# Column strips of the modulation products, chained into whole groups on TensorE

## Chip, core and metric

The kernel runs on one core of a Trainium2 chip. The metric is the device time of one execution in microseconds. Three timed runs of the kernel before gave 1551.01, 1553.77 and 1553.95 us; their median, 1553.77 us, is the time that the change is held against.

## What is computed

Two models run one after the other on the same 256 tokens of width 1024. The first block has two layers of four parallel mixers (latent attention, differential attention, a top-k attention, a short convolution), each between a normalisation, an input projection and an output projection. The second block has two layers with a mixer and a mixture of 16 experts; its shifts, scales and gates come from a *modulation* vector, which depends on the inputs `c` and `c_ctx` alone:

```python
def second_block(x, c, ctx, c_ctx, ada_w, ada_b, ...):
    silu_c = jax.nn.silu(c)
    silu_cc = jax.nn.silu(c_ctx)
    x_lat, x_ctx = x, ctx
    for l in range(DEPTH):
        mod_lat = (silu_c @ ada_w[l] + ada_b[l])[:, None, :]
        mod_ctx = (silu_cc @ ada_w[l] + ada_b[l])[None, None, :]
        sh1, sc1, g1, sh2, sc2, g2 = jnp.split(mod_lat, 6, axis=-1)
...
def reference(...):
    x = first_block(...)
    return second_block(x, ...)
```

Two rows (`c` and `c_ctx`) go through a 1024 x 6144 matrix in each of two layers: much weight, little arithmetic.

## The kernel before

The program is written with a tile framework whose scheduler simulates the engines and takes, on each engine, the ready instruction that stands first in priority; each engine then runs its instructions strictly in the order in which they were put. An order edge (`issue_after`) says only that one instruction stands behind another on its engine. `high_priority(n)` moves what it encloses n places ahead in priority.

**First block.** Weights come in units of 128 x 2048 float32 (1 MB) into a ring of three buffers called `w` (`stream`, L353). Each unit is split by ScalarE (`wh`, L373) and VectorE (`wl`, L374) into a high and a low part, and TensorE multiplies high by high, high by low and low by high (`mm3`): these are the `pf` and `pt` products of the input and output projections. Between them stand the products of the mixers: `ixp`, `uq`, `ukv`, `lgA`, `lgB`, `poA` and others.

**Modulation.** The weights of the modulation, 48 loads of 1 MB, go through the same ring (`wload`, L347). The generator `ada_chunks` (L941) loads one such buffer for each k and issues four products from it. Each has the 32 columns of `cT` as its stationary operand (two of them in use) and 512 columns of weight moving, and writes another 32 partitions of one PSUM bank: the four products stand in four column strips of TensorE's array. Two k are summed in the bank and then added to `adab` by VectorE (L952). The generator is drawn from by `fill` (L966) at 12 places of each first layer, one step of two k at each, as work for TensorE between the mixers' products. In the kernel before, the four products of a buffer are issued by a plain loop, with no edge between them:

```python
for t in range(4):
    self.mm(ps[32 * t:32 * t + 32], self.cT[:, k], w[:, t], k % ADAK == 0, k % ADAK == ADAK - 1)
```

so the scheduler is free to put another ready product between two strips.

**Groups that were chained already.** `side_by_side` (L274) issues the products of several streams, interleaved, with an order edge from each to the next, for products that stand in different strips of the array or in different rows of it: `cmb`, `lgN`, `poN` and `lgC` in the second block's first mixer (L1210 to L1342), `yc` in the last mixture of experts (L1993). Within each round the streams are issued in falling order (`reversed(group)`). The edges keep the order, not the neighbourhood: other products may stand in between.

After the first block come the second block's first mixer (neighbourhood attention and an mLSTM, some 400 to 760 us), a mixture of experts with gathered rows (to some 1085 us), the second mixer and the last mixture of experts.

Of the kernel before, what the change touches and what calls it, by code (L numbers as in the profile page):

```python
# [31 lines left out]
XBUFS = 3  # L32
ADA = "pj"
FILLP = 1
MIX = (1, 1, 0, 0)
XL = (0, 1)
XN = (lambda nc: nc.gpsimd, lambda nc: nc.gpsimd)
ADAK = 2
# [196 lines left out]
class Emit:  # L235
# [37 lines left out]
    def side_by_side(self, *streams, banks=(), after=None):  # L273

        one = self.cst["ones"][:, :1]
        for m in [(b[:1, :1], one, one, True, True) for b in banks] + [m for group in zip(*streams) for m in reversed(group)]:
            with self.tc.issue_after(after) if after else ExitStack():
                after = self.mm(*m).ins  # L280
        return after

# [652 lines left out]
    def ada_chunks(self, pool):  # L935

        nc, io = self.nc, self.io
        for l in range(2):
            ab = pool.tile([P, 3, 512], F32, tag="adab", name="adab")
            with self.tc.issue_after(self.rooted):  # L940
                nc.gpsimd.memset(ab, 0.0)  # L941
                for w in range(2):
                    nc.gpsimd.dma_start(ab[w:P:32], io["ada_b"][l])
            for m in range(3):
                for k in range(KD):
                    if k % ADAK == 0:
                        ps = self.psum(ADA, name="ada")
                    w = self.wload(io["ada_w"][l, m, :, k], [P, 4, 512])
                    for t in range(4):
                        self.mm(ps[32 * t:32 * t + 32], self.cT[:, k], w[:, t], k % ADAK == 0, k % ADAK == ADAK - 1)  # L950
                    if k % ADAK == ADAK - 1:
                        nc.vector.tensor_add(ab[:, m], ps, ab[:, m])  # L952
                    if k == KD - 1 and m == 2:
                        for w in range(2):
                            v = self.mod[l][w:w + 1].rearrange("o (m t j) -> (o t) m j", m=3, t=4)
                            nc.gpsimd.dma_start(v, ab[w:P:32])
                    if k % 2:
                        yield

    def fill(self, n=1):  # L960
        for _ in range(n):
            with self.tc.high_priority(FILLP):
                next(self.filler, None)
# [923 lines left out]
    def moe_onehot(self, l, NT):  # L1887
# [4 lines left out]
        with ExitStack() as ctx:  # L1892
# [89 lines left out]
            def back(pr, owT, Y, after=None):  # L1982
                for t in range(NT):

                    pos = [self.psum(POT[j], name="yc") for j in range(2)]
                    r = [slice(64 * j, 64 * j + 64) for j in range(2)]
                    after = self.side_by_side(*([(pos[j], owT[r[j], t, i], Y[i][n][r[j]], i + n == 0, i + n == 2)
                                                 for i in range(2) for n in range(2)] for j in range(2)), after=after)
                    for j in range(2):
                        js = slice(j * 512, (j + 1) * 512)  # L1990
                        o = self.x[:, t, js]
                        nc.vector.tensor_add(o, o, pos[j])  # L1992
                        if pr == NE // 2 - 1:  # L1993
                            (nc.sync, nc.scalar)[j].dma_start(self.out[t * P:(t + 1) * P, js], o)
# [4 lines left out]
            for e, (w13, w2) in enumerate(weights):  # L1999
                pr = e // 2  # L2000
                ph = self.psum("pj", name="ph")
                if e == NE - 1:
                    step = second(e - 1, *todo)
                    for k in range(0, KD, 2):
                        last = hidden(e, tiles[pr][0], w13, k, ph, 2)
                        if k == 0:
                            back(pr - 1, tiles[pr - 1][1], Ys[-2:], last.ins)
                        for _ in range(MIX[k // 2]):
                            with self.tc.issue_after(last.ins):
# [82 lines left out]
```

## Time and profile before

| | before |
|---|---|
| median of three timed runs | 1553.77 us |
| the profiled execution | 1563.38 us, span 1561.6 us |
| TensorE (PE) busy | 1413.6 us, 91% |
| VectorE (DVE) busy | 716.0 us, 46% |
| ScalarE (ACT) busy | 438.9 us, 28% |
| GpSimd (POOL) busy | 158.0 us, 10% |
| modulation products (`ada`), union of their spans | 73.2 us |
| mean granted TensorE clock | 0.945 of full speed |
| weight loads of the modulation | 48 of 1024 KB, 4.9 us to landing |

The profiled execution took 1563.38 us, 0.6% more than the median. The page gives busy time as the union of the spans of an engine's instructions. Matmuls are pipelined and their ends are modelled, so the length of one product says little; what one costs is read from the start of one to the start of the next. A float32 product leaves two records in the trace: 192 `ada` products are 384 records.

### The profile page before, as it was taken

What the parts mean: (1) busy time and instruction counts of PE and PEld (TensorE: products, weight loads), DVE (VectorE), ACT (ScalarE), POOL (GpSimd) and SP (SyncE); (2) the same over time, 40 slices, a digit from 0 to 9 for tenths busy, and PEclk for the clock granted to TensorE, in tenths of its full rate; (3) what the DMA queues carried; (4) which work ended last, traced back from release to release, by engine and by line L of the source; (5) the groups of instructions that cost most, each with busy time, mean ns of one, the idle gap of its engine ahead of it and who ended that gap; (6) DMA issues with size and microseconds to landing.
All of it is one profiled execution on the core that took longest, in us unless ns stands there. A gap on an engine that the chain in (4) does not pass through costs nothing.

```text
span 1561.6 us, 24557 instructions
## 1 busy us (share of the span) xinstructions
PE 1413.6 (91%) x10118; PEld 926.5 (59%) x10118; DVE 716.0 (46%) x1609; ACT 438.9 (28%) x881; POOL 158.0 (10%) x217
## 2 busy tenths in 40 slices
PE   8999999999999998989569999888538998999997
PEld 7576787768888994959523333333138685443442
DVE  4756545856654546365511111111076655333433
ACT  4334332344543324243201111111034442111110
POOL 2100120002100221000110000000143000000000
PEclk9999999999999996999789999999759998999998
DMA  8677675676623111205589888777553517999990
GB/s 295 233 295 285 229 252 174 233 276 237 217 84 96 55 55 39 70 28 216 217 302 330 300 305 338 287 304 300 199 221 109 222 38 284 421 421 422 380 405 31
DMA packets 65703, 359.23 MB, mean 230 GB/s; under 512 B 13027, under 2 KB 16349, under 8 KB 26793
## 3 DMA queue, kind: packets, MB, share of 16 engines
q1 hardware_dynamic: 57680, 335.04, 57.5%
q0 software_dynamic: 5824, 19.68, 3.9%
q10 hardware_dynamic: 2073, 2.79, 0.5%
q8 instruction: 84, 1.38, 0.4%
q14 instruction: 42, 0.34, 0.1%
HBM read 344.77 MB, written 12.71 MB: 229 GB/s over the span
## 4 chain that ended last, share of the span: by engine, by line
PE 35%; DMA 8%; DVE 3%; issue 2%; ACT 1%; POOL 1%; SPq 0%; ACTq 0%; POOLq 0%; DVEq 0%
PE ph L270 13%; PE py L270 6%; DMA w<-in_w_dram 5%; PE pt L270 4%; PE pq L270 3%; DMA ybuf<-ysq 2%; PE gtp L294 1%; PE yc L270 1%; PE px L270 1%; PE pyq L270 1%; PE lgG L270 1%; PE poG L270 1%; PE xtp L294 1%; DMA X<-hbuf,tab 1%; DVE x L1992 1%
## 5 line engine op out<-in xcount | busy, mean ns | idle before, releaser
L270 PE MATMUL ph<-w,XT 128*64 128x512 f32 x1024 | 250.6, 611 | 17.8 <-DMA w<-in_w_dram 14.9
L374 DVE TENSOR_TENSOR wl<-w,wh 128x2048 fp32r<-128x2048 f32 (+2 forms) x74 | 151.8, 2058 | 87.1 <-ACT wh L373 86.8
L270 PE MATMUL pt<-wh,hT 128*128 128x256 f32 x640 | 185.0, 290 | 3.5 <-ACT wh L373 2.0
L270 PE MATMUL pt<-wl,hT 128*128 128x256 f32 x640 | 184.0, 289 | 0.0
L270 PE MATMUL pt<-wh,hTl 128*128 128x256 f32 x640 | 183.2, 290 | 0.6 <-DVE hTl L374 0.2
L373 ACT CAST wh<-w 128x2048 fp32r<-128x2048 f32 (+2 forms) x74 | 126.6, 1719 | 122.9 <-PE pt L270 44.9
L270 PEld LDWEIGHTS ph<-w,XT 128*64 128x64 f32 x1024 | 71.2, 138 | 139.6 <-issue 120.0
L270 PE MATMUL pf<-hTl,wh 128*128 128x256 f32 (+1 forms) x480 | 141.6, 296 | 0.0
L270 PE MATMUL pf<-hT,wh 128*128 128x256 f32 (+1 forms) x480 | 141.3, 298 | 0.3
L270 PE MATMUL pf<-hT,wl 128*128 128x256 f32 (+1 forms) x480 | 140.3, 293 | 0.7 <-DVE wl L374 0.7
L1758 DVE SCALAR_TENSOR_TENSOR ga<-ga,ph 64x512 f32<-64x512 f32 x32 | 21.8, 680 | 258.8 <-ACT ga L1757 258.8
L270 PEld LDWEIGHTS pt<-wh,hT 128*128 128x128 f32 x640 | 123.2, 193 | 9.6 <-ACT wh L373 2.5
L270 PEld LDWEIGHTS pt<-wl,hT 128*128 128x128 f32 x640 | 123.0, 192 | 4.6 <-issue 3.4
L270 PEld LDWEIGHTS pt<-wh,hTl 128*128 128x128 f32 x640 | 121.7, 192 | 5.2 <-issue 3.8
L270 PE MATMUL py<-w,gT 128*64 128x512 f32 x512 | 121.8, 605 | 0.8 <-DVE gT L1831 0.8
L270 PEld LDWEIGHTS pf<-hT,wh 128*128 128x128 f32 x480 | 91.5, 192 | 11.1 <-issue 4.7
L270 PEld LDWEIGHTS pf<-hT,wl 128*128 128x128 f32 x480 | 92.0, 192 | 6.8 <-issue 2.7
L270 PEld LDWEIGHTS pf<-hTl,wh 128*128 128x128 f32 x480 | 92.1, 192 | 5.6 <-issue 4.4
L270 PEld LDWEIGHTS py<-w,gT 128*64 128x64 f32 x512 | 36.1, 138 | 68.5 <-issue 65.2
L270 PE MATMUL ada<-w,cT 128*32 128x512 f32 x384 | 73.2, 612 | 1.3 <-DMA w<-in_ada_w_dram 1.3
L270 PE MATMUL pq<-w,XT 128*32 128x256 f32 x1024 | 72.1, 386 | 0.0
L270 PE MATMUL pt<-wh,yT 128*128 128x256 f32 x256 | 63.7, 293 | 0.0
(527 smaller groups left out, 2139.7 us busy)
## 6 DMA issues: line engine op xcount, KB each, us to landing
w<-in_w_dram SPq DMA_DIRECT2D x192, 1024.0 KB, 15.5
w<-in_ada_w_dram SPq DMA_DIRECT2D x48, 1024.0 KB, 4.9
w<-in_w_in_dram SPq DMA_DIRECT2D x30, 1024.0 KB, 6.9
w<-in_even_w_dram SPq DMA_DIRECT2D x12, 1024.0 KB, 6.2
w<-in_w_out_dram SPq DMA_DIRECT2D x8, 1024.0 KB, 5.0
w<-in_even_out_dram SPq DMA_DIRECT2D x4, 1024.0 KB
ybuf<-ysb SPq DMA_DIRECT2D x16, 256.0 KB
w<-in_odd_w_dram SPq DMA_DIRECT2D x4, 1024.0 KB
```

What stands on the lines that cost most here:

```text
L270: self.last = self.nc.tensor.matmul(out, lhsT, rhs, start=start, stop=stop)
L294: self.nc.tensor.transpose(out, in_, self.cst["ident"][:k, :k])
L373: self.nc.scalar.copy(hi, src)
L374: (self.nc.vector if eng == "v" else self.nc.gpsimd).tensor_tensor(out=lo, in0=src, in1=hi.bitcast(F32), op=ALU.subtract)
L1758: nc.vector.scalar_tensor_tensor(g, g, 1.0, ph[0:n], op0=ALU.add, op1=ALU.mult)
L1992: nc.vector.tensor_add(o, o, pos[j])
```

## The change

The four products of a modulation buffer go through `side_by_side`: an order edge from each to the next, in falling order of the strips. And in `side_by_side`, for all its callers, every product behind the first of a group is lifted by 20000 places in priority, so that a group once begun is taken on as soon as its next product is ready.

```diff
+GROUPP = 20000
...
         one = self.cst["ones"][:, :1]
-        for m in [(b[:1, :1], one, one, True, True) for b in banks] + [m for group in zip(*streams) for m in reversed(group)]:
-            with self.tc.issue_after(after) if after else ExitStack():
+        ms = [(b[:1, :1], one, one, True, True) for b in banks] + [m for group in zip(*streams) for m in reversed(group)]
+        for n, m in enumerate(ms):
+            with ExitStack() as c:
+                if after:
+                    c.enter_context(self.tc.issue_after(after))
+                if n:
+                    c.enter_context(self.tc.high_priority(GROUPP))
                 after = self.mm(*m).ins
         return after
...
                     w = self.wload(io["ada_w"][l, m, :, k], [P, 4, 512])
-                    for t in range(4):
-                        self.mm(ps[32 * t:32 * t + 32], self.cT[:, k], w[:, t], k % ADAK == 0, k % ADAK == ADAK - 1)
+                    self.side_by_side(*([(ps[32 * t:32 * t + 32], self.cT[:, k], w[:, t], k % ADAK == 0, k % ADAK == ADAK - 1)]
+                                        for t in range(4)))
```

No product, load or copy is added or removed. What moves is the order. On TensorE, in the first layer's latent attention (`ixp`, `uq` and `ukv` are its and the top-k attention's products; the number behind `w_` is the buffer's), the kernel before has

```order
L270 MATMUL ada_518<-w_519,cT_116 32x512
L270 MATMUL ixp_532<-s4a_364,s2a_459 128x512
L270 MATMUL ada_518<-w_519,cT_116 32x512 x3
L270 MATMUL ada_518<-w_525,cT_116 32x512
L270 MATMUL ixp_544<-s4a_364,s2a_459 128x512
L270 MATMUL ada_518<-w_525,cT_116 32x512 x3
L270 MATMUL ada_658<-w_659,cT_116 32x512
L270 MATMUL uq_673<-s8a_204,wuq_154 128x256
L270 MATMUL ada_658<-w_659,cT_116 32x512
L270 MATMUL uq_673<-s8a_204,wuq_154 128x256
```

and the changed kernel at the same place

```order
L271 MATMUL ada_518<-w_519,cT_116 32x512 x4
L271 MATMUL ixp_532<-s4a_364,s2a_459 128x512
L271 MATMUL ada_518<-w_525,cT_116 32x512 x4
L271 MATMUL ixp_544<-s4a_364,s2a_459 128x512
L271 MATMUL ada_658<-w_659,cT_116 32x512 x4
L271 MATMUL uq_673<-s8a_204,wuq_154 128x256 x4
```

The strips of one buffer now stand together, and the four `uq` products behind them too. Over the whole program the 192 products stood in 61 uninterrupted runs: 22 of one product, 4 of two, 8 of three, 18 of four, 2 of five and 7 of eight. Now they stand in 37 runs: 26 of four and 11 of eight (two buffers behind each other).

On TensorE at the start of the first output projection (`pf` is a product of the input projection, `pt` of the output projection), the kernel before has, of the eight strips of two buffers, one among `pf` products further ahead and the other seven in five runs:

```order
L270 MATMUL pf<-hT,wl 128x256
L270 MATMUL ada<-w,cT 32x512 x2
L270 MATMUL pt<-wh,yT 128x256
L270 MATMUL ada<-w,cT 32x512 x2
L270 MATMUL pt<-wl,yT 128x256
L270 MATMUL pt<-wh,yTl 128x256
L270 MATMUL ada<-w,cT 32x512
L270 MATMUL pt<-wh,yT 128x256
L270 MATMUL ada<-w,cT 32x512
L270 MATMUL pt<-wl,yT 128x256
L270 MATMUL ada<-w,cT 32x512
L270 MATMUL pt<-wh,yTl 128x256
```

and the changed kernel

```order
L271 MATMUL pf<-hTl,wh 128x256
L271 MATMUL pf<-hT,wl 128x256
L271 MATMUL ada<-w,cT 32x512 x4
L271 MATMUL pt<-wh,yT 128x256
L271 MATMUL pt<-wl,yT 128x256
```

One buffer's four strips stand whole ahead of the projection; the other buffer's four stand where the single strip stood before. The order of the weight loads on SyncE's queue is the same up to the end of the first block. In the second block the `yc` products stand in 25 runs where there were 27, one group of four `lgC` is cut into one and three, and `pt`, `qk` and `pom` products of the first mixer change places.

## Rows read from the trace of the kernel before

**Rows 1.** Page, the span in 40 equal slices, busy tenths of TensorE.

```profile
PE   8999999999999998989569999888538998999997
```

**Rows 2.** Windows by stage: length, busy us of each engine, granted clock, DMA share, GB/s.

```profile
0.00:405.00 405.00, 393.77 (x2667) 292.37 (x2668) 242.57 (x597) 157.28 (x282) 49.05 (x74) 0.99 0.71 250
...
560.00:780.00 220.00, 188.92 (x1360) 153.63 (x1358) 123.46 (x318) 73.32 (x168) 25.21 (x34) 0.89 0.29 106
780.00:1085.00 305.00, 279.65 (x2324) 109.64 (x2324) 45.73 (x86) 35.90 (x84) 15.52 (x16) 0.95 0.84 311
1085.00:1561.00 476.00, 397.88 (x2564) 231.60 (x2562) 217.60 (x436) 114.23 (x240) 43.22 (x48) 0.91 0.66 261
```

**Rows 3.** Waits of TensorE from 20 to 405 us: total, times, longest.

```profile
PE htp L270 <- ACT idx L315: 3.5, 2, 3.3
PE ada L270 <- DMA w<-in_ada_w_dram: 1.3, 1, 1.3
```

**Rows 4.** Timeline of TensorE, first layer: start us, us, instructions, records.

```profile
45.82 1.05 PE L270 MATMUL ada<-w,cT 128*32 128x512 f32 x2
46.79 1.12 PE L270 MATMUL ixp<-s4a,s2a 128*128 128x512 f32 x2
47.85 1.07 PE L270 MATMUL ada<-w,cT 128*32 128x512 f32 x8
48.84 1.12 PE L270 MATMUL ixp<-s4a,s2a 128*128 128x512 f32 x2
...
50.90 0.70 PE L270 MATMUL uq<-s8a,wuq 128*128 128x256 f32 x2
51.52 1.05 PE L270 MATMUL ada<-w,cT 128*32 128x512 f32 x2
52.50 0.70 PE L270 MATMUL uq<-s8a,wuq 128*128 128x256 f32 x2
...
57.96 1.89 PE L270 MATMUL uq<-s8a,wuq 128*128 128x256 f32 x8
59.78 1.06 PE L270 MATMUL ada<-w,cT 128*32 128x512 f32 x8
```

**Rows 5.** The same timeline, two buffers behind each other.

```profile
71.82 1.92 PE L270 MATMUL ada<-w,cT 128*32 128x512 f32 x16
73.68 0.33 PE L294 MATMUL ptp<-cpack,p 128*128 128x128 f32 x1
```

**Rows 6.** The same timeline, three strips and the fourth, among projection products.

```profile
114.44 1.06 PE L270 MATMUL ada<-w,cT 128*32 128x512 f32 x6
115.43 0.38 PE L270 MATMUL pf<-hT,wh 128*128 128x256 f32 x1
115.74 1.05 PE L270 MATMUL ada<-w,cT 128*32 128x512 f32 x2
116.72 0.38 PE L270 MATMUL pf<-hTl,wh 128*128 128x256 f32 x1
116.94 0.28 PE L270 MATMUL pf<-hT,wl 128*128 128x256 f32 x1
117.06 0.28 PE L270 MATMUL pf<-hT,wh 128*128 128x256 f32 x1
```

**Rows 7.** The same timeline, a group behind an idle stretch, and one that waited.

```profile
224.53 1.94 PE L270 MATMUL ada<-w,cT 128*32 128x512 f32 x8
226.39 1.22 PE L270 MATMUL htp<-idx,x 128*128 128x128 f32 x4
...
338.47 1.06 PE L270 MATMUL ada<-w,cT 128*32 128x512 f32 x8 [1.27 <-DMA w<-in_ada_w_dram]
```

**Rows 8.** Windows of 5 us, columns as in rows 2.

```profile
65.00:70.00 5.00, 5.00 (x20) 3.12 (x20) 4.97 (x23) 2.27 (x9) 0.14 (x1) 1.00 0.19 79
...
80.00:85.00 5.00, 5.00 (x44) 5.00 (x44) 5.00 (x7) 1.58 (x1) 0.00 (x0) 1.00 1.02 424
```

**Rows 9.** Waits of all engines from 20 to 405 us.

```profile
ACT wh L373 <- DMA w<-in_w_in_dram: 21.8, 8, 5.6
```

**Rows 10.** Waits of SyncE's queue up to 420 us.

```profile
SPq L362 <- PE ada L270: 87.8, 27, 11.6
```

## Prediction, made before the changed kernel ran

> **What bounds the kernel now.** I read the page's slices first: TensorE is at eight or nine tenths almost everywhere [rows 1]. The windows by stage say where that means something. The first block, up to some 405 us, keeps TensorE busy for 393.8 of 405 us at a granted clock of 0.99 [rows 2], 2.4 GHz nearly throughout, while VectorE works 243 us, ScalarE 157 us and the DMA engines 71% of the time. What TensorE waits for there, by the view of waits, comes to little: 3.5 us on ScalarE at the start of the second layer and a single wait of 1.3 us on a modulation load [rows 3]. So the first block is TensorE's own queue: a microsecond taken out of it ends the block a microsecond earlier, as long as the other engines and the loads keep up. Busy alone would not show that, since ends of matmuls are modelled; the waits do. The stages behind, from 560 us, have idle TensorE time in each, 31, 25 and 78 us by the same windows [rows 2], and follow on the first block's result.
>
> The modulation products are all in the first block. What one costs depends on its neighbours. One strip alone: from 51.52 to the next instruction at 52.50, 0.98 us [rows 4]. Four strips together: from 47.85 to 48.84, 0.99 us [rows 4]. Three: 0.99 us, and the fourth, cut off by one `pf` product, another 0.98 us [rows 6]. Eight, that is two buffers: 71.82 to 73.68, 1.86 us [rows 5]. A run of one to four strips costs the same: strips that stand together run at the same time, and a strip alone takes the time of four.
>
> **The change, term by term.** *Fewer runs.* The order counts 22, 4, 8, 18, 2 and 7 runs of one, two, three, four, five and eight. From these rows I price one and two at 0.98, three and four at 0.99, five and eight at 1.86 us: 26 x 0.98 + 26 x 0.99 + 9 x 1.86 = 68.0 us. Now 26 runs of four and 11 of eight: 25.7 + 20.5 = 46.2 us. The difference is **21.8 us** less. (Two runs were longer than their price, the one at half the clock, 1.86 us for four strips, and the one that waited [rows 7]; I leave both as they are.)
>
> *Fewer switches.* A run also slows what is next to it. From the `pf` at 115.43 to the second `pf` behind the strip, 116.94, it is 1.51 us [rows 6]; take off the run of 0.98 and two ordinary steps of 0.12 (116.94 to 117.06), and 0.29 us are left for going in and out. Among `uq`: from 50.90 to 52.50 it is 1.60 us; the run is 0.98, one `uq` product among its own is a quarter of 57.96 to 59.78, 0.46 [rows 4], which leaves 0.16. There are 24 runs fewer (61 to 37): 3.8 to 7.0 us, of which I take the middle, **5.4 us**, since both neighbourhoods are common.
>
> *The falling order of the strips, and the edges.* No instruction and no semaphore wait that the profile shows. Taken as nothing; the price if the overlap suffers is a rival below. The Trainium skill (TensorE: Matmul & The Clock Gate, Why this matters for your kernels) speaks against a full gain: three column tiles of 512 columns ran 2.38 times as fast as one after the other, not three times. By that figure, an estimate, a group would cost 3 x 0.98 / 2.38 = 1.23 us and not 0.99, and the changed runs some 59 us, so that 9 of the 21.8 us were left. The trace disagrees: three strips took 0.99 us against 0.98 for one [rows 6], 2.97 times; I go by the rows.
>
> *What loses its cover.* 27.2 us go out of a block in which VectorE, ScalarE and the loads do the same work as before. Averages leave room: VectorE would be at 243 of some 378 us, the DMA engines at 0.76. But there are tight places. Around 65 to 85 us VectorE works through the top-k search, 4.97 to 5.00 of each 5 us [rows 8]; TensorE has to come to its results some 5 us earlier there, and most of the chain in front of them also starts earlier, since the `uq` products that it waits for are no longer spread among strips. The DMA engines swing between 79 and 424 GB/s in the same stretch [rows 8]: loads go out when a ring buffer comes free, often by an `ada` product itself (27 waits of the queue for it, 87.8 us in all [rows 10]), and then three go at once. ScalarE's casts waited 21.8 us for projection weights [rows 9], all of it hidden behind queued products. Where two buffers are now used in one run, the second load has to be there 1 us after the first. Bounds: below, the one wait of 1.3 us goes too (a gain); above, each of the other 10 runs of eight waits like the one at 338.47 [rows 7], 10 x 1.27 = 12.7 us of loss. One of seven such runs waited so far, so the nearest row speaks for some 2 us, and I add as much for VectorE: **4 us** of loss.
>
> *The second block.* The groups that were chained before gain no work and lose none; the two runs of `yc` that go are worth at most 2 x 0.29 us in a stage with 78 us of idle TensorE time, taken as nothing. The changed places of `pt`, `qk` and `pom` in the first mixer can cost or give back some of the 31 us that TensorE idles there [rows 2]; a tenth of it, 3 us either way, is my estimate, and zero my value. Everything behind the first block waits for its result, and the weights of the experts for buffers that the first mixer frees, so I expect the stages to move as a whole: the DMA engines run at 0.29 from 560 to 780 us [rows 2], so no stream runs ahead there that would stay where it is.
>
> **Sum:** 21.8 + 5.4 - 4 = 23.2 us less. The profiled execution took 1563.4 us, so it would come to 1540.2; the median of the timed runs lies 0.6% below, which changes 23.2 by 0.1, so the timed kernel should take 1553.8 - 23 = **1531 us**. A difference of 0.2%, 3 us, is about what a measurement of this kernel can tell from none.
>
> **Rivals.**
> *The cover runs out (0.14).* Loads or VectorE's searches end last in more places than I allow and take back about half: 10 runs of eight at 1.27 us each, 1553.8 - 27.2 + 12.7 = 1539 us, up to 1549. For it: the swings of the DMA engines and VectorE's full stretches [rows 8]. Against it: one load wait in 48 groups so far [rows 3], and a gain spread over 380 us.
> *The strips overlap only in part in falling order (0.06).* A group then costs between 0.99 us and the 0.98 us of each strip alone. At a quarter more, 1.23 us, the sum is 1553.8 - 9 - 5.4 + 4 = 1543 us; were the overlap lost altogether, 144 more strips at nearly 1 us each would make it slower by over 100 us, which I give no share. The Trainium skill's 2.38 (the page named above) would be this case. Against it: three strips in 0.99 us [rows 6], if in rising order.
> *The gain is given back later (0.04).* A stage behind ends by something that did not move, and the time stays at 1554 us. For it: the expert stage runs at 311 GB/s with DMA share 0.84 [rows 2]. Against it: its loads start from buffers that the mixer in front frees.
> *Slower: the ring of weight buffers becomes the bound (0.04).* TensorE runs in order, so a group that stands whole before its load has landed holds up everything behind it, where a single strip further back did not yet have to start. It decides if the mean wait of the 48 groups exceeds 27.2 / 48 = 0.57 us; if each of the 37 runs waited 1.27 us as at 338.47 [rows 7], that is 47 us and the kernel takes 1574 us. Against it: the DMA share of 0.71 [rows 2].
>
> **Chances and range.** My forecast, with a gain of 15 to 32 us, has 0.72. Faster by over 0.2% are it and the first two rivals, 0.92; within 0.2% the third, 0.04; slower the last, 0.04. The range runs from 1521 us (no wait added, the upper price of switches, 3 us gained in the mixer: 21.8 + 7.0 + 1.3 + 3 = 33) to 1546 us, which takes in the partial overlap and most of the case where the cover runs out.
>
> **What would show it.** The 384 `ada` records in 37 runs, each run of four at 0.99 us from its start to the next instruction and each of eight at 1.86; their union down from 73.2 to about 50 us; the first block's end near 382 us with TensorE still busy in nearly all of it; the stages behind as long as before. Wrong would be: records of one group that start half a microsecond apart (no overlap); waits of `ada` on its load, or of `pf` and `pt` on `wl`, of more than 10 us in the first block; or a first block shorter by 23 us with an end that is not.

## The result, and the profile after

The changed kernel took 1535.83 us (median of five runs, 1533.85 to 1542.31) against 1553.77 us before: 0.9889 times, 95% interval 0.9858 to 0.9921. The prediction was 1531.0 us, 1521 to 1546. The profiled execution took 1533.85 us, span 1532.1 us.

The slices of the page, as [rows 1], and the windows by stage, as [rows 2] (the first stage now ends at 385, the others are 20 us earlier):

```profile
PE   8999989999899998989399999888358998999997
```

```profile
0.00:385.00 385.00, 370.81 (x2677) 290.81 (x2678) 240.70 (x595) 154.05 (x276) 46.40 (x72) 0.99 0.72 263
540.00:760.00 220.00, 185.20 (x1364) 153.24 (x1362) 124.44 (x321) 73.49 (x168) 25.25 (x35) 0.91 0.29 106
760.00:1065.00 305.00, 283.20 (x2349) 110.97 (x2349) 48.44 (x93) 37.34 (x88) 15.40 (x16) 0.97 0.84 315
1065.00:1532.00 467.00, 389.98 (x2537) 228.74 (x2537) 214.91 (x429) 112.42 (x236) 43.17 (x48) 0.91 0.67 264
```

The same work now fits in a first stage that is 20 us shorter, with TensorE idle for 14 us of it (385 less 370.8) where it was 11. DMA share and GB/s rose little: the loads follow the ring.

The `ada` products come in the 37 runs that the order showed. The timeline of TensorE at the places of [rows 4] and [rows 5], one run that waited, and the half-clock run that answers to [rows 7]:

```profile
47.85 1.07 PE L271 MATMUL ada<-w,cT 128*32 128x512 f32 x8
48.84 1.13 PE L271 MATMUL ixp<-s4a,s2a 128*128 128x512 f32 x2
...
51.06 1.99 PE L271 MATMUL uq<-s8a,wuq 128*128 128x256 f32 x8
...
68.32 1.92 PE L271 MATMUL ada<-w,cT 128*32 128x512 f32 x16
70.18 0.92 PE L271 MATMUL lgA<-ks,qs 128*128 128x128 f32 x4
...
120.49 1.06 PE L271 MATMUL ada<-w,cT 128*32 128x512 f32 x8
122.78 1.06 PE L271 MATMUL ada<-w,cT 128*32 128x512 f32 x8 [1.23 <-DMA w<-in_ada_w_dram]
...
218.95 1.94 PE L271 MATMUL ada<-w,cT 128*32 128x512 f32 x8
220.82 1.22 PE L271 MATMUL htp<-idx,x 128*128 128x128 f32 x4
```

A run of four costs 0.99 us from start to next, one of eight 1.86. At 122.78 the second buffer of a run of eight came late. The four `uq` products stand together at 51.06, as the order said.

What TensorE waits for from 20 to 385 us, the counterpart of [rows 3]:

```profile
PE htp L271 <- ACT idx L321: 3.3, 1, 3.3
PE ada L271 <- DMA w<-in_ada_w_dram: 2.5, 3, 1.2
PE pt L271 <- DVE wl L380: 2.0, 2, 1.2
PE pf L271 <- DVE wl L380: 0.5, 1, 0.5
```

Two things are new: three waits for modulation loads where there was one (two of them inside runs of eight, for the second buffer, as the prediction feared), and waits of the output projection (`pt`) for `wl`, the low parts of its weights, where there was none. (The second layer's projection lies behind 385 us and has two more; the page's costliest groups put 4.0 us of idle time ahead of `pt<-wl,yT` to `wl` over the whole program, 3.2 of it up to 420 us.)

### The profile page after: what moved, and what is told of

The parts are those of the page before. It is cut to its first block, busy times and chain, and to the rows that moved or that the text cites. A ratio compares the mean times of both kernels' runs of the same rounds, so it can differ in the third digit from the quotient of the medians.

```text
span 1532.1 us, 24552 instructions
## 1 busy us (share of the span) xinstructions
PE 1380.1 (90%) x10118; PEld 919.8 (60%) x10118; DVE 714.3 (47%) x1609; ACT 438.1 (29%) x881; POOL 154.2 (10%) x217
## 4 chain that ended last, share of the span: by engine, by line
PE 35%; DMA 8%; DVE 3%; ACT 1%; issue 1%; POOL 1%; SPq 1%; ACTq 0%; POOLq 0%; DVEq 0%
PE ph L271 14%; PE py L271 6%; DMA w<-in_w_dram 5%; PE pt L271 4%; PE pq L271 3%; DMA ybuf<-ysq 3%; PE yc L271 1%; PE gtp L300 1%; PE px L271 1%; PE pyq L271 1%; PE lgG L271 1%; PE poG L271 1%; PE xtp L300 1%; DVE x L1998 1%; ACT wh L379 0%
## 5 line engine op out<-in xcount | busy, mean ns | idle before, releaser
L271 PEld LDWEIGHTS pt<-wh,hT 128*128 128x128 f32 x640 | 123.4, 193 | 10.6 <-issue 4.2
L271 PE MATMUL pt<-wl,yT 128*128 128x256 f32 x192 | 54.6, 286 | 4.0 <-DVE wl L380 4.0
```

The source lines that it names most:

```text
L271: self.last = self.nc.tensor.matmul(out, lhsT, rhs, start=start, stop=stop)
```

## Where the time went: a landmark

The `mg` products stand early in the second block and wait for the first block's result. Their start splits an execution in two. The rows of that tile (minimum, median and maximum length in ns, first and last start in us), for the kernel before in two executions and the changed kernel, one fence each:

```profile
L270 PE MATMUL mg<-hT,wmg x64: 272/273/297, 464.2 to 467.4; 128*32 128x128 f32 x64
```

```profile
L270 PE MATMUL mg<-hT,wmg x64: 272/273/297, 462.4 to 465.6; 128*32 128x128 f32 x64
```

```profile
L271 PE MATMUL mg<-hT,wmg x64: 272/273/297, 444.6 to 447.8; 128*32 128x128 f32 x64
```

All runs with this landmark, but for resident, which stands with its experiment; "behind" is the span of the profiled execution less the start of `mg`. Each ratio is to runs of the kernel before on the same chip.

| kernel | median (range), us | ratio [95%] | `mg` | behind |
|---|---|---|---|---|
| before, first profile | 1553.77 | | 464.2 | 1097.4 |
| before_again | 1555.42 (1549.0 to 1561.2) | 1.0000 [0.9979, 1.0021] | 462.4 | 1088.9 |
| changed | 1535.83 (1533.9 to 1542.3) | 0.9889 [0.9858, 0.9921] | 444.6 | 1087.5 |
| after_again | 1537.49 (1532.2 to 1543.9) | 0.9883 [0.9846, 0.9920] | 446.3 | 1088.4 |
| edges_only | 1558.69 (1553.3 to 1564.4) | 1.0014 [0.9990, 1.0038] | 464.0 | 1095.4 |
| lift_only | 1554.82 (1552.2 to 1562.9) | 1.0000 [0.9978, 1.0021] | 461.5 | 1090.0 |
| cover | 1548.08 (1545.3 to 1553.7) | 0.9965 [0.9946, 0.9984] | 454.0 | 1091.0 |
| no_edges | 1543.01 (1537.1 to 1549.5) | 0.9931 [0.9905, 0.9957] | 444.6 | 1102.0 |
| first_only | 1533.43 (1532.5 to 1534.9) | 0.9872 [0.9856, 0.9887] | 444.0 | 1088.6 |
| rising | 1542.35 (1537.6 to 1544.6) | 0.9922 [0.9905, 0.9938] | 445.0 | 1097.9 |
| cover2 | 1539.12 (1534.3 to 1545.8) | 0.9916 [0.9893, 0.9939] | 444.9 | 1091.8 |
| lift_no_edge | 1537.97 (1537.2 to 1538.9) | 0.9899 [0.9883, 0.9916] | 444.3 | 1091.1 |

The changed kernel reaches `mg` 16.1 to 19.6 us earlier, by either pair of profiles. What lies behind stays at 1087.5 to 1088.9 us in three of these four profiles; the first profile of the kernel before was long there, and the kernel before alone thus shows 1089 and 1097 us. So the gain is the first block's. A single `mg` is good to some 3 us: before, before_again and lift_only have the same order in the first block, and their `mg` runs from 461.5 to 464.2.

## Experiments

**The two kernels again.** No edit.

> The unchanged kernel before. The two profiles compared so far differ by 29.5 us of span while the timed medians differ by 17.9 us, and the profile of before was 9.6 us above its median. Theory: the change is worth 19 to 20 us in the first block (start of the first gate product mg at 464.2 us before, 444.6 after) and nothing behind it, and the profile of before was simply a long execution in its later stages. Then this profile has mg again within 1 us of 464.2 us, 61 ada runs, and a span near 1552 us, the difference of some 9 us to the first profile lying behind 470 us. Rival: the change also shortens the later stages by some 10 us; then this profile's stages behind 470 us are as long as in the first profile of before (1097 us from mg to the end). Ratio of times: 1.00 within 0.003 by either.

> The changed kernel again. Theory: mg within 1 us of 444.6 us, 37 ada runs, time 1533 to 1540 us, ratio 0.987 to 0.991; what varies from run to run lies behind the first block. Rival (the change acts on the later stages too): the stretch from mg to the end stays at 1087 us or below, where before has 1097.

Measured: table. The times and the counts of runs came out as expected; `mg` missed the 1 us that was allowed, 1.8 us early in before_again and 1.7 us late in after_again. The rival, later stages shortened by the change, fell: before_again has 1088.9 us behind `mg`. In before_again the 61 runs took 68.8 us in sum, each counted from its start to the next instruction, with no wait; in the changed kernel the 37 runs took 49.7, of which 2.1 are waits for loads. (The third load wait, 0.3 us, stands ahead of a run and not in it.) Without waits that is 68.8 - 47.6 = 21.2 us. (After_again: 48.2 less 0.9.)

**Another group that was cut.** The order shown ahead of the prediction leaves out that other groups of the first block changed too, and one of these changes costs time. `poC` adds up two heads in two column strips of 64. In before_again the four products of two heads stand together; in the first layer of the changed kernel both such groups are cut in two. One of them, in before_again and in the changed kernel:

```profile
168.21 0.88 PE L270 MATMUL poC<-PT,vbc 128*64 128x256 f32 x8
169.02 0.76 PE L294 MATMUL ptp<-cpack,p 128*128 128x128 f32 x5
```

```profile
160.56 0.86 PE L271 MATMUL poC<-PT,vbc 128*64 128x256 f32 x4
161.36 0.33 PE L300 MATMUL ptp<-cpack,p 128*128 128x128 f32 x1
161.62 0.86 PE L271 MATMUL poC<-PT,vbc 128*64 128x256 f32 x4
```

Four together take 0.81 us, two alone 0.80. So these strips behave as those of `ada`, and the two cuts cost 1.6 us, here and in after_again, first_only and edges_only (experiments below); in no_edges, rising, lift_no_edge and cover2 the groups of `poC` are whole.

**One part alone: chain without lift, and lift without chain.**

Edges_only has nothing lifted, and lift_only has the loop of the kernel before for the modulation.

```diff
-GROUPP = 20000
+GROUPP = 0
...
-                if n:
+                if n and GROUPP:
```

```diff
-                    self.side_by_side(*([(ps[32 * t:32 * t + 32], self.cT[:, k], w[:, t], k % ADAK == 0, k % ADAK == ADAK - 1)]
-                                        for t in range(4)))
+                    for t in range(4):
+                        self.mm(ps[32 * t:32 * t + 32], self.cT[:, k], w[:, t], k % ADAK == 0, k % ADAK == ADAK - 1)
```

> The chain of order edges without the lift in priority (the ada products in side_by_side, no high_priority). The order has 55 runs (17 of one, 1 of two, 10 of three, 15 of four, 4 of five, 1 of seven, 7 of eight). Theory, that each run costs 0.98 us for up to four strips, 1.86 for up to eight, and some 0.2 for going in and out: 17.6 + 24.8 + 22.3 = 64.7 us of runs against 68.0, 6 switches fewer (1.2 us), so 4 to 5 us less than before, about 1549 us, ratio 0.997. Rival, that the edges do the work and the lift little: 1540 us or below. Rival, that the falling order of the strips costs or gains by itself: a run of four differs from 0.99 us by more than 0.03.

> The lift in priority for the groups that were chained before (cmb, lgN, poN, lgC, yc); the modulation products as in the kernel before, in 61 runs. Theory: the lift of the old groups is worth nothing, 1554 us, ratio 1.000 within 0.003, mg at 464 us. Rival, that the gain behind the first block comes from the lift of the old groups: 1544 to 1549 us, with mg at 464 us and a shorter stretch behind it.

Lift_only came as expected: the lift of the older groups alone is worth nothing. Edges_only missed: 4 to 5 us less was expected, and it is not faster. Its waits from 20 to 464 us show why (the two that before_again does not have there):

```profile
PE ada L271 <- DMA w<-in_ada_w_dram: 2.5, 1, 2.5
PE pt L271 <- DVE wl L380: 2.4, 2, 1.2
```

Without waits its 55 runs took 3.1 us less than the 61 of before_again (68.1 - 2.5 = 65.6 against 68.8). Against that, TensorE's idle time up to `mg` grew by 3.9 us, and the cut groups of `poC` cost 1.6. The loss of cover is paid here nearly without the gain. (By `mg` it is 1.6 us worse than before_again, which is within what single executions differ by.) An edge keeps the order of four strips; it does not bring them together.

**The edges taken away, the lift kept.**

No_edges issues the strips from a plain loop; rising keeps the chain but turns the order of the strips around.

```diff
-                    self.side_by_side(*([(ps[32 * t:32 * t + 32], self.cT[:, k], w[:, t], k % ADAK == 0, k % ADAK == ADAK - 1)]
-                                        for t in range(4)))
+                    for t in range(4):
+                        with self.tc.high_priority(GROUPP) if t else ExitStack():
+                            self.mm(ps[32 * t:32 * t + 32], self.cT[:, k], w[:, t], k % ADAK == 0, k % ADAK == ADAK - 1)
```

```diff
-                                        for t in range(4)))
+                                        for t in reversed(range(4))))
```

> The four products of a modulation buffer come from a plain loop as in the kernel before, with no edge between them and in no falling order; only the lift of the second to fourth product stays (and the lift of the older groups). 39 whole runs, 30 of four and 9 of eight, price 46.4 us against 46.3 of the changed kernel. If whole groups are what brings the gain, edges and falling order are worth nothing: 1536, within 1.5 us of the changed kernel. If the falling order matters for the overlap of the strips, or the edges themselves for the time of a run, runs of four differ from 0.99 us and the time moves by 37 times that difference: at 1.23 us, 9 us more.

> As the changed kernel, but the strips of a modulation buffer are issued in rising order; chain and lift stay. The order of all instructions by name is that of the no_edges kernel on every engine, 39 runs, 30 of four and 9 of eight. If falling order or edges make a run shorter, this differs from no_edges or its runs of four from 0.99 us. If neither matters and no_edges lost its 7 us to another order of the second block, this kernel loses them too: mg starts at 444.6 and the time is 1543, within 2 us of no_edges.

In both, `mg` starts at 444.6 and 445.0 and every run of four that met neither a wait nor the half clock took 0.99 to 1.00 us. So the first block gains the same with or without edges, in falling or rising order: the lift alone makes whole groups. (That `mg` agrees to within 1 us is a sum of several parts: against the changed kernel these two keep `poC` whole, 1.6 us less, and take 1.8 us more for `lgB` and `poB`.) But both kernels took 1542 to 1543 us, which the theory "only the runs matter" did not expect of no_edges. The loss lies behind `mg` (1102.0 and 1097.9 us), where the order of the second block had changed as well. Their intervals touch that of the changed kernel, and the kernel before alone differs by 8.5 us behind `mg` between two executions, so single profiles carry little here.

**The order of the second block.** First_only lifts the modulation groups and leaves the older groups as they were; its second block stands on TensorE as in the kernel before, but for a few rows. Lift_no_edge is no_edges with `side_by_side` as in the kernel before, so that the older groups are not lifted.

```diff
-                if n:
+                if n and lift:
                     c.enter_context(self.tc.high_priority(GROUPP))
...
-                                        for t in range(4)))
+                                        for t in range(4)), lift=True)
```

> The modulation groups are chained and lifted as in the changed kernel; the older groups (cmb, lgN, poN, lgC, yc) are not lifted. On TensorE the first block stands row for row as in the changed kernel and the second block as in the kernel before, but for a few rows. If the whole gain is the first block's and the order of the second block is worth nothing, mg starts at 444.6 us as in the changed kernel and the time is 1536, within 2 us of it. If the no_edges run was slower because the order of its second block is worse, orders of the second block are worth some 7 us, and this kernel can stand as far from the changed kernel to either side: 1529 to 1543, with mg still at 444.6.

> The least change that makes whole groups: the plain loop of the kernel before, no edges, the second to fourth product of a buffer lifted; side_by_side as in the kernel before. On TensorE the first block stands row for row as in the rising kernel (39 runs); in the second block some 160 rows stand otherwise than in the first_only kernel, among them the last products of the logits and of the gated sums in the second mixer (lgG, gtp, poG) and of the last mixture of experts (ph, yc), which stand as in no_edges and rising; the first mixer's stand nearly as in first_only. mg starts at 444.6 to 445. If the 7 us of no_edges and rising come from the lift of the older groups in the first mixer, they go: 1534. If they come from the order in the second mixer and behind it, they stay: 1541 to 1543, with the gap opening behind 1088 us.

First_only takes 1533.43 us: the whole gain without the second part of the change. Its interval does not overlap those of no_edges and rising; it overlaps that of the changed kernel, so the two are not told apart. Lift_no_edge, at 1537.97, fell between its two expectations, and its interval overlaps those of first_only, no_edges and rising alike: what part of the loss goes with the lift of the older groups is not shown. What TensorE waits for from 680 us on, the rows that differ most, first_only, then no_edges, then one row of rising:

```profile
PE xtp L300 <- DMA X<-hbuf,tab: 9.1, 1, 9.1
...
PE px L271 <- DVE wn L1519: 1.5, 1, 1.5
...
PE lgG L271 <- ACT ne L1487: 1.2, 1, 1.2
```

```profile
PE xtp L300 <- DMA X<-hbuf,tab: 14.3, 1, 14.3
...
PE px L271 <- DVE wn L1520: 2.7, 1, 2.7
PE lgG L271 <- ACT ne L1488: 2.6, 2, 1.8
```

```profile
PE xtp L300 <- DMA X<-hbuf,tab: 10.6, 1, 10.6
```

The gathered rows of the first mixture of experts (`X`) came 5.2 us later for `xtp`; `px` and `lgG`, whose neighbours stand in another order, waited 2.6 us more. That is 7.8 of the 13.4 us between these two profiles behind `mg`, but the profiled no_edges was also a long one, 5.4 us above its median. The 2.6 us are the same in rising, which has the order of no_edges. The gather wait is not: 14.3 us in no_edges and 10.6 in rising, 13.8 and 11.0 in the two profiles of the kernel before. So it varies by some 3 us with the order unchanged, and what part of the 5.2 us is the order's is not shown. The rest of the difference was not settled.

**What sets the waits of `pt` for `wl`.** The chain in the changed kernel, in the timelines of ScalarE, VectorE and TensorE at the first output projection:

```profile
183.61 1.90 ACT L379 CAST wh<-w 128x2048 fp32r<-128x2048 f32 x1 [4.99 <-PE pf L271]
...
185.54 2.29 DVE L380 TENSOR_TENSOR wl<-w,wh 128x2048 fp32r<-128x2048 f32 x1
...
183.62 1.07 PE L271 MATMUL ada<-w,cT 128*32 128x512 f32 x8
184.61 0.38 PE L271 MATMUL pt<-wh,yT 128*128 128x256 f32 x1
...
187.89 0.39 PE L271 MATMUL pt<-wl,yT 128*128 128x256 f32 x1 [0.74 <-DVE wl L380]
```

The last `pf` product frees a buffer of the high parts; ScalarE's cast and VectorE's subtraction then take 1.90 and 2.29 us, and only then has TensorE the next unit's low part, 4.3 us after 183.61. Its own work in between, one group and some `pt` products, ran out 0.74 us before. In before_again five short runs stood there:

```profile
186.97 1.05 PE L270 MATMUL ada<-w,cT 128*32 128x512 f32 x4
...
188.27 1.05 PE L270 MATMUL ada<-w,cT 128*32 128x512 f32 x4
...
189.68 1.05 PE L270 MATMUL ada<-w,cT 128*32 128x512 f32 x2
...
190.98 1.04 PE L270 MATMUL ada<-w,cT 128*32 128x512 f32 x2
...
192.27 1.04 PE L270 MATMUL ada<-w,cT 128*32 128x512 f32 x2
```

Three experiments asked whether loads or casts bind there. In resident the products read a tile that is already in SBUF, so no modulation weights are loaded (the line below; the tile is also loaded in the first layer instead of the second, and the stationary operand is 64 times smaller):

```diff
-                    w = self.wload(io["ada_w"][l, m, :, k], [P, 4, 512])
+                    w = self.xc.rearrange("p a (b c) -> p (a b) c", b=2)
```

> The modulation products read a tile that is in SBUF already, so the 48 modulation loads are gone (48 MB less, and no ring buffer held by them); the values are not the modulation's. 30 runs, 12 of four and 18 of eight, price 45.4 us by the rows of before, 0.9 less than the changed kernel. If the lost cover is the loads' (waits of ada on its load, projection weights late because modulation loads share the ring), waits of ada go to zero and the pt waits on wl go too: about 1529, 5 to 7 us less than the changed kernel. If it is the two-buffer chain of casts in the output projection, the pt waits on wl stay at some 4 us, and only the 1.1 us of load waits and the 0.9 us of runs go: about 1534.

Only the first block of this run is read: behind it other values send tokens to other experts, and products that the changed kernel never reaches (1536 records of `dy`) stretch the span to 5554.1 us. `mg` starts at 442.6, 2.0 us earlier than in the changed kernel: the size that the theory of casts gave (1.1 + 0.9) and not the 5 to 7 of the other. That the size fits is luck in part: against this execution of the changed kernel the runs gave 0.5 us and the waits 1.9, and other products, with `poA` and `poC` cut once more, took 0.4 back. What decides is which waits are left. No wait of `ada` for a load is left; of `pt`, up to 420 us:

```profile
PE pt L271 <- DVE adab L958: 1.3, 2, 0.7
PE pt L271 <- DVE wl L380: 1.2, 1, 1.2
```

With 48 MB less to load the projection still waits 2.5 of the 3.2 us, part of it now put down to the addition of the modulation sums, which stands right behind `wl` on VectorE. So most of these waits are not the loads'.

Cover and cover2 give the output projection modulation work in other places. In both the generator gives out one buffer at a time. Cover's edit is below; cover2 has one buffer behind the first unit, three ahead of the projection and none at the start of the convolution.

```diff
-        self.fill()
...
+            if c < 2:
+                with self.tc.issue_after(self.last.ins), self.tc.high_priority(FILLP):
+                    next(self.filler, None)
```

> The modulation work of two k that stood ahead of each first layer's output projection is given out one buffer at a time behind the first and the second projection unit, as a whole group of four each; still 37 runs, 26 of four and 11 of eight. If the 4.0 us that TensorE waits for the low parts of the projection weights (pt on wl, four waits of 0.6 to 1.4 us in the two output projections) come from the single strips that no longer stand between those products, whole groups in their place take most of it back: the four waits shrink to under 1.5 us in sum and the kernel takes about 1533, 2 to 4 us less than the changed kernel. If those waits are set by ScalarE and VectorE alone (the casts end when they end, whatever TensorE does in between), what the groups cover is waited for later, and the time stays within 1 us of the changed kernel's 1536.

> The two buffers of modulation work that stood at the start of each first layer's convolution are moved: one joins the two ahead of the output projection, one stands as a whole group behind the first projection unit. 36 runs, 24 of four and 12 of eight, price 46.1 us against 46.3. In the cover run the two waits for yT, 3.5 us each, came since nothing stood ahead of the output projection any more; here they stay away. If the waits of pt on wl in the output projections (3.2 to 4.0 us in the changed kernel, 0.7 and 1.2 us in each layer) are a matter of what stands beside the casts, they shrink to under 1 us in sum and mg starts 2 to 4 us earlier, at 441 to 443 us. If work moved out of the convolution opens a wait there that it hid, mg stays at 444 to 446. The time of the whole is as uncertain as the second block's order, 7 us.

Cover missed, and by much: 12 us slower than the changed kernel, with 37 runs as cheap as there. The waits for `wl` are gone, but the work taken away had covered the convolution's last result, `yT`. TensorE's longest wait up to 420 us, the timeline, and the window behind it:

```profile
PE pt L271 <- ACT yT L379: 7.1, 2, 3.5
```

```profile
188.02 0.58 PE L271 MATMUL pt<-wh,yT 128*128 128x256 f32 x1 [3.53 <-ACT yT L379]
188.40 0.41 PE L271 MATMUL pt<-wl,yT 128*128 128x256 f32 x1
...
194.20 0.29 PE L271 MATMUL pt<-wl,yT 128*128 128x256 f32 x1
```

```profile
188.00:194.40 6.40, 6.38 (x30) 6.37 (x30) 0.76 (x2) 0.30 (x1) 0.00 (x0) 0.52 0.34 143
```

Behind the wait of 3.53 us the granted clock is 0.52, the 1.2 GHz level, for 6.4 us; the 27 steps from 188.40 to 194.20 take 0.215 us each instead of 0.12 [rows 6], 2.6 us more. Two layers: 7.1 of waits and 5.2 of clock, less the 3.2 of `wl` waits that went, is 9.1 us, against 9.4 by `mg`; the rest of the 12 us lies behind `mg` and was not looked into.

In cover2, `yT` is covered again and `mg` stands at 444.9: no gain. `pt` still waits 3.3 us for `wl` and 1.1 us for `wh`, and in the second layer some 1.4 us more went to a stretch at half the clock behind these waits (the last section has its rows). Moving the modulation work does not take the waits away. The chain of two casts above is what is left as their cause; that its two buffers set its pace was not shown, since a third pair was not tried.

## Why the prediction was right, and where its sum was off

*The place.* Right. The first block was TensorE's own queue; what came out of it came off the end, and the stages behind moved as a whole.

*Fewer runs, 21.8 us.* Measured 21.2, without waits. Runs cost what [rows 4 to 6] said; two runs of eight that a wait broke took 0.2 us more each beside the wait. The Trainium skill (TensorE: Matmul & The Clock Gate, Why this matters for your kernels) gives 2.38 times for three column tiles. The runs here disagree: every undisturbed run of four at full clock took 0.99 to 1.00 us against 0.98 for one strip, 3.9 times for four strips.

*Falling order and edges, nothing.* Right for the time of a run, which is the same in no_edges, rising and lift_no_edge; all three reach `mg` within 1 us of first_only.

*Loss of cover, 4 us.* Too small, and wrong in its composition, though within its bounds. The step named loads and VectorE's top-k search. Against before_again, modulation loads cost 2.5 us (1.2 in after_again) and the output projection's casts 3.2, and the waits at the entry to the second block (`hT`, `hfull`, `cT`) grew by some 0.6: 6.3 us from 20 us on. TensorE's idle time over the whole stretch up to `mg` grew from 12.2 to 18.3 us, 6.1. VectorE's search cost nothing that the waits show. I had seen five short runs among the `pt` products in the order and priced them as waste alone; they had covered the 4.3 us of casts.

*Fewer switches, 5.4 us.* Too large, and the step left something out. `mg` moved 17.7 us between before_again and the changed kernel. With 21.2 for the runs and 6.1 for the idle time, 2.6 us are left for all other products. Counted from start to start without idle time, `uq` came 1.5 us cheaper, `pt` 1.3 and `pf` 1.0: 3.8 us, the lower bound of the step, among the products between which the removed runs had stood. The cut groups of `poC` took 1.6 us of it, a term that the sum did not have; the other products gave 0.4. After_again has the same 3.8 and 1.6. The upper price was misread: the `pf` at 115.43 stands between two runs [rows 6], so its 0.29 us hold the way out of the run of three as well. In before_again the way in costs 0.09 us (0.21 between the two rows below, where 0.12 is ordinary) and the way out 0.10 (116.72 to 116.94 in [rows 6]): 0.19 for a run, 4.6 us for 24.

```profile
151.60 0.28 PE L270 MATMUL pf<-hT,wl 128*128 128x256 f32 x1
151.81 1.06 PE L270 MATMUL ada<-w,cT 128*32 128x512 f32 x8
```

*The second block, 0 ± 3.* Zero held for this change, but the bounds were too narrow for the kind of edit: kernels that reach `mg` within 1 us of each other, with other orders behind it, gave 1533.4 to 1543.0 us.

So 21.2 + 3.8 - 1.6 + 0.4 - 6.1 = 17.7 us instead of 23.2; the medians differ by 17.9. The errors did not cancel: runs, switches, the cut groups and the cover all came out worse than forecast, and the wide bounds kept the time inside. *The rivals.* That the cover runs out had part of the truth: some 6 us came back, where it needed 12.7. Partial overlap, a gain given back later and a ring that becomes the bound fell. The stages behind are as long as before.

## What to carry to other kernels

Strips that can share the array must stand next to each other in the issued order: an edge between them does not do it alone, a lift of the later ones does. Look for other such groups that the new order cuts: here two groups of `poC` lost 1.6 us that way. Work spread out as filler also covers something; before gathering it, look at what the engine would wait for at each place that it leaves, the casts of the next weight unit and the last result of the stage included. Where a scheduler decides, an edge or a lift also reorders places that the edit did not mean; first_only, which leaves the older groups as they stand, gave the whole gain without that part.

## What the runs showed of the hardware that was not expected

A wait can cost nearly twice its length: 3.53 us without work on TensorE were followed by 6.4 us at the 1.2 GHz level, 2.6 us more (cover, in both layers nearly alike). The waits of 0.7 and 1.2 us at the same projection in the changed kernel were followed by a granted clock of 1.00:

```profile
188.00:194.00 6.00, 6.00 (x51) 6.00 (x52) 1.96 (x5) 0.74 (x2) 0.55 (x1) 1.00 0.69 251
198.70:204.00 5.30, 5.26 (x44) 5.26 (x45) 2.88 (x2) 0.67 (x1) 0.00 (x0) 1.00 0.77 249
```

The length of one wait does not tell it, though. In cover2 each layer's output projection waits some 0.5 us and then 1.51 us. In the first layer the clock stays at 1.00 behind it; in the second it is 0.52 for 3.3 us:

```profile
186.52 0.39 PE L271 MATMUL pt<-wl,yT 128*128 128x256 f32 x1 [1.51 <-DVE wl L380]
...
383.73 0.58 PE L271 MATMUL pt<-wl,yT 128*128 128x256 f32 x1 [1.51 <-DVE wl L380]
```

```profile
186.50:190.00 3.50, 3.48 (x29) 3.48 (x30) 0.64 (x2) 0.00 (x0) 0.00 (x0) 1.00 0.88 311
...
383.70:387.00 3.30, 3.27 (x15) 3.27 (x16) 0.65 (x2) 1.16 (x4) 1.48 (x4) 0.52 0.98 225
```

What makes the difference was not settled. The half-clock group of [rows 7] at 224.53 stands behind TensorE's wait of 3.3 us for `idx` [rows 3]. Behind that wait the stretch at half the clock is nearly 7 us long in before_again and 3.4 us in rising.
